# Two copies that spread the rotary table are issued earlier, and their temporaries are held longer

## The chip, the cores and the metric

The kernel runs on one core of a Trainium2 chip. The metric is device time in microseconds (us) of one execution, as the median of several. The core has five engines that each work through a queue of their own, in order: TensorE (PE; its loading of the stationary operand is shown apart as PEld), VectorE (DVE), ScalarE (ACT), GpSimd (POOL) and SyncE (SP), which here issues the transfers. They meet through semaphores alone, so that an instruction that waits holds up everything behind it on its engine.

## The reference

Two decoder layers of the same form run over 512 tokens with 1024 features. In each layer one input projection gives the queries, keys and values of two groups of heads and of an indexer. The first group (kind "a" in the kernel) attends to a sliding window with a learned sink; the second (kind "b") attends only to those keys that the indexer ranks highest, 128 a query. Both groups are projected back, then come a normalisation, a gated feed-forward part with a small second input, and a normalisation.

```python
h = x @ w_in
qa, ka, va, qb, kb, vb, qi, ki, wi = jnp.split(h, cuts, axis=-1)
qa = rope(qa.reshape(B, S, SWA_KV_HEADS, SWA_G, HEAD_DIM), positions)
...
ki = rope(layer_norm(ki, idx_k_g, idx_k_b), positions)
...
sc = jnp.einsum('bqhd,bsd->bqhs', qib, ki).astype(jnp.float32)
idx_score = jnp.einsum('bqhs,bqh->bqs', jax.nn.relu(sc), wib.astype(jnp.float32))
...
_, sel = lax.top_k(idx_score, k_top)
...
mix = jnp.concatenate([oa, ob], axis=-1) @ w_o
x = layer_norm(DN_ALPHA * x + mix, ln1_g, ln1_b)
```

`rope` rotates the two halves of each head by an angle that depends on the token's position and on the feature; its cosines and sines are the rotary table. The table is the same for both layers.

## The kernel before

**Tiles.** The 512 tokens are four blocks (NT = 4) of 128. An fp32 product is made of three fp32r matmuls (`mm3`, L334 to L336) of a high and a low part of each operand. Weights come by SP's transfers into three staging tiles (`wst`); ScalarE rounds each to its high part (L280, L287) and GpSimd subtracts to get the low part (L281, L288), into a ring of five (`wsp`). PSUM has eight banks that go round in a few rings: accumulators, two for transposes (`tp`) and two for scores (`sc`). `t2k()` gives one of twelve temporaries of 128 x 512 fp32, `slot()` one of 28 tiles.

**Start of a layer.** `start()` does, in this order: for each of the four blocks the indexer's projection of 296 columns (`gi_out` rotates its parts, `turns` transposes them, L620 to L622); then for pairs of blocks the projection of 384 columns with keys and values (`kv_out` rotates the keys: a product with the table on VectorE, L520, an addition on GpSimd, L522, a rounding on ScalarE, L525, a subtraction on GpSimd, L526; and copies the values on ScalarE, L613); then `turned_tables()`; then the queries, whose features lie on partitions, so that their rotation (`q_out`, L645) needs the table transposed.

**The table.** `tab64` holds cosines and sines with tokens on partitions and is made once. `turned_tables()` makes the transposed form in each layer: for each of the two halves ScalarE copies 32 columns a block four times side by side into a temporary (L632), PE transposes its four 128 x 128 pieces (L636), and ScalarE copies the bank into the tile `lng` (L637), whose two halves are what `q_out` reads.

**Beside it.** `index()` runs interleaved with `start()`: eight scores a block on PE (L677), a ReLU on ScalarE (L679), a weighted sum on VectorE (L680), for blocks 1 to 3. `topk()` follows, for the same three blocks: 16 rounds each of a maximum of eight (L691) and their replacement (L692) on VectorE, over 256, 384 or 512 keys, 48 rounds a layer. `attention()` runs over units of a block and a group of heads: `scores` (PE L716, VectorE's mask and row maximum L720, ScalarE's exponential L724, the sum's reciprocal on VectorE L730, GpSimd's spreading of it L732) and `values` (transposes of the exponentials L753, transposes of the reciprocals L764, products with the values L747, L772). `rest()` gives the remaining queries and the first part of the output projection (L822, L824 add it to the residual).

**What sets the order.** Several such generators run side by side; each yields an estimate of its cost on PE, and a planner (`order.run`) gives the next turn to the one that is behind by these costs; `order.later` puts transposes off until a due time. From the order in which instructions are issued in this way, a scheduler that knows the tiles' dependencies settles the order on each engine before the kernel runs. A table that is issued at another place thus also changes what stands beside what further on.

Of the kernel before, what the change touches and what calls it, by code (L numbers as in the profile page):

```python
# [20 lines left out]
NT = S // 128  # L21
# [75 lines left out]
def hybrid_kernel(ctx: ExitStack, tc: tile.TileContext, x, p, positions, ln_in_g, ln_in_b, w_in,  # L97
# [3 lines left out]
    PE, V, A, G, SP = nc.tensor, nc.vector, nc.scalar, nc.gpsimd, nc.sync  # L101
# [11 lines left out]
    def bank(tag, bufs, dt=F32):  # L113
        return psum.tile([128, 512], dt, name="bank", tag="bank", bufs=8)

    def acc():
        return bank("acc", 4)
# [4 lines left out]
    def t2k(dt=F32):  # L122
        return tmp.tile([128, 512], dt, name="t2k", tag="t2k")
# [23 lines left out]
    idf = const.tile([128, 128], F32, name="idf")  # L147
# [172 lines left out]
    def w_take():  # L320
        i = wpos["use"]
        if wq[i][0] == "raw":
            i += 1
        wpos["use"] = i + 1
        assert i in w_live, (i, wpos)
        return w_live.pop(i)

    def w_rel():
        wpos["room"] += 1
        w_pump()  # L330

    def mm3(o, sh, sl, mh, ml, start, stop, again=False):

        PE.matmul(o, sh, mh, start=start, stop=False, skip_group_check=again)  # L334
        PE.matmul(o, sh, ml, start=False, stop=False, skip_group_check=again)  # L335
        PE.matmul(o, sl, mh, start=False, stop=stop, skip_group_check=again)  # L336
# [15 lines left out]
    for i in range(4):  # L352
        ps = bank("gb", 4)
# [3 lines left out]
    def tok(t):  # L357
        return slice(t * 128, (t + 1) * 128)
# [30 lines left out]
    def ln_in_sums(t):  # L389
        total, mean = sm(1, "lnsum1"), sm(1, "lnm")  # L390
        A.activation(t2k().bitcast(BF16), xt[t], AF.Copy, accum_out=total)
        A.mul(mean, total, -1.0 / D)
        stats[t] = mean, squares(t, mean)

    def ln_in(t):
        halves = [xt[t][:, h * 512:(h + 1) * 512] for h in range(2)]
        if t == 0:
            mv = sm(2, "bmv")
            for h in range(2):
                ln_stats(t, h)  # L400
            V.bn_aggr(mv, stats.pop(t))
            mean, var, of = mv[:, 0:1], mv[:, 1:2], 1
        else:
            (mean, var), of = stats.pop(t), D
        for h, c in enumerate(halves):
            V.scalar_tensor_tensor(c, c, mean, gb_in[h], op0=OP.add if t else OP.subtract, op1=OP.mult)
        rs = rstd_of(var, of=of)
        for h, c in enumerate(halves):
            last["norm"] = V.scalar_tensor_tensor(c, c, rs, gb_in[2 + h], op0=OP.mult, op1=OP.add).ins
# [24 lines left out]
    def behind(ins, fn):  # L434

        def f(*args):
            with tc.issue_after(ins):
                fn(*args)
        return f

    def to_features(t):
        ts = slice(t * 128, (t + 1) * 128)
        for j in range(KT // 4):
            ps = bank("tp", 2)
            for i in range(4):
                k = 4 * j + i
                PE.transpose(ps[:, i * 128:(i + 1) * 128], xt[t][:, k * 128:(k + 1) * 128], idf)  # L447
            pv = ps.rearrange("p (a n) -> p a n", a=4)
            last["copy"] = A.copy(fh[:, 4 * j:4 * j + 4, ts], pv).ins  # L449
            V.tensor_tensor(fl[:, 4 * j:4 * j + 4, ts], pv, fh[:, 4 * j:4 * j + 4, ts], OP.subtract)  # L450
# [3 lines left out]
    tab64 = const.tile([128, NT, 2, 64], F32, name="tab64")  # L454
# [86 lines left out]
    def take(n):  # L541
        return [w_take() for _ in range(n)]

    def project(ws, n, blocks, lhs, done, rel=0):

        ks = [(i, r, len(w[0])) for i, w in enumerate(ws) for r in range(len(w[0]))]
        ps = [acc() for _ in blocks]
        for k, (i, r, a) in enumerate(ks):
            for o, t in zip(ps, blocks):
                mm3(o[:, :n], *lhs(t, k), ws[i][0][r], ws[i][1][r], k == 0, k == len(ks) - 1)  # L550
            if i < rel and r == a - 1:
                w_rel()
            yield 3 * len(blocks) * 0.218 * n / 512
        for o, t in zip(ps, blocks):
            done(t, o)

    for l in range(L):
# [1 line left out]
        kiT = slot()  # L559
        qiT, qT, work, wi, vt, ma = {}, {}, {}, {}, {}, {}  # L560
        ready = set()
        kin, kmv, turned = {}, {}, []

        def gi_out(t, ps):

# [39 lines left out]
        def kv_out(t, ps):  # L605
# [18 lines left out]
                order.tick(0.4)  # L624
            order.later(D_K, turns)

        def turned_tables():

            cs = const.tile([128, D], F32, name="lng", tag="lng")
            for i in range(2):  # L630
                wide = t2k()
                A.copy(wide.rearrange("p (t n i) -> p t n i", t=NT, n=4),  # L632
                       tab64[:, :, i, None, :32].to_broadcast([128, NT, 4, 32]))
                ps = bank("tp", 2)
                for t in range(NT):
                    PE.transpose(ps[:, tok(t)], wide[:, tok(t)], idf)  # L636
                A.copy(cs[:, i * 512:(i + 1) * 512], ps)  # L637
            return cs[:, :512], cs[:, 512:]

# [193 lines left out]
        def queries(kind, g):  # L833
            ps = [acc(), acc()]
            for k in range(KT):
                if k % 4 == 0:
                    w = w_take()
                for u in range(2):
                    mm3(ps[u], w[0][k % 4][u], w[1][k % 4][u], fh[:, k], fl[:, k], k == 0, k == KT - 1)
                if k % 4 == 3:  # L840
                    w_rel()
                yield 6 * 0.227
            q_out(kind, g, ps)

        def start():
            ws = take(3)
            for t in range(NT):
                if l == 0 or t == 3:
                    to_features(t)
                    yield 0.9  # L850
                if l == 0 and t == 0:
                    with tc.issue_after(last["copy"]):
                        ln_in_sums(2)
                    ln_in_sums(3)
                    for _ in table:
                        pass
                if l == 0 and t + 1 < NT:
                    ln_in(t + 1)
                done = gi_out
                if l == 0 and t + 1 < NT:  # L860
                    done = behind(last["norm"], gi_out)
                if l == 0 and t == 2:
                    with tc.issue_after(last["norm"]):
                        V.tensor_scalar(nsink, sink, -1.0, None, op0=OP.mult)
                yield from project(ws, 296, (t,), from_f, done, 3 * (t == 3))
            ws = take(4)
            for b in ALL:
                yield from project(ws, 384, b, from_f, kv_out, 4 * (b is ALL[-1]))
            turned.extend(turned_tables())
            for q in QS[:NSTART]:  # L870
                yield from queries(*q)

        def rest():
# [5 lines left out]
            for h in range(2):  # L879
                ws = take(2)  # L880
                for b in ALL:
                    yield from project(ws, 512, b, from_ma, res_out(h, ALPHA), 2 * (b is ALL[-1]))

        order.run((start(), 1.0), (index(), 1.0), credit=False)
        order.run((rest(), R_MAIN), (attention(), 1.0), (topk(), R_TOP))
        order.flush()
# [118 lines left out]
        for gi, fs in enumerate(GROUPS):  # L1005
            hs = []
            for f in fs:
# [7 lines left out]
                if gi == 1 and f == fs[0]:  # L1015
                    pT = {}
                    for k in range(2):
                        ps = bank("tp", 2)
# [14 lines left out]
            for h in range(2):  # L1033
                ps = [acc() for _ in range(NT)]
                n = len(hs)
# [13 lines left out]
        for b in TAIL:  # L1049
            for h in range(2):  # L1050
# [4 lines left out]
                ps = [acc() for _ in b]  # L1055
# [52 lines left out]
```

## Time and profile before

| | us |
|---|---|
| median of 3 runs | 1276.74 (1276.61 to 1277.25) |
| the profiled execution | 1275.16 |
| its span, first to last instruction | 1273.4 |
| PE busy in the span | 1223.8 (96%) |
| VectorE busy | 773.4 (61%) |
| GpSimd busy | 677.9 (53%) |
| ScalarE busy | 583.4 (46%) |

The mean clock granted to TensorE is 0.985 of full speed. Busy shares are means over stages that differ: in the page's 40 slices VectorE is between 30% and 90% and above. In the profile, a line such as L636 names the line of the kernel that issued the instruction, `out<-in` names tiles, and the bracket behind an instruction gives the idle time of the engine just before it and what ended it.

### The profile page before, as it was taken

The page shows a single profiled execution, that of the slowest core. Times are in us where ns is not written, and L with a number is a line of the kernel's source. Part 1 is how long each engine was busy: PE and PEld are TensorE (multiplying, and loading weights), DVE is VectorE, ACT ScalarE, POOL GpSimd, SP SyncE. Part 2 cuts the span into 40 slices and gives each one's busy share as a digit, 9 for nine tenths or more (in the row PEclk, how much of TensorE's full clock was granted, in tenths as well). Part 3 has the DMA queues.
Part 4 walks back from the last instruction along what each step waited for, and adds up shares of the span by engine and source line. Part 5 has one row for each costly group of instructions (what it writes and reads, how often), then busy time and mean ns, then how long its engine had stood idle before and what let it go on. Part 6 is the DMA issues. An engine that isn't in the chain of part 4 may idle for free.

```text
span 1273.4 us, 17210 instructions
## 1 busy us (share of the span) xinstructions
PE 1223.8 (96%) x6056; PEld 1006.3 (79%) x6056; DVE 773.4 (61%) x1678; ACT 583.4 (46%) x1185; POOL 677.9 (53%) x523
## 2 busy tenths in 40 slices
PE   7889999999999999999997989999999999999996
PEld 5877667888888888888896867679888888888885
DVE  7689953773636363726677997556736363645365
ACT  6557774443434343434335766843434342434331
POOL 6856632366565656562166645324756575747400
PEclk9989999999999999999998989999999999999998
DMA  5324241343242323034032433204242423231321
GB/s 174 85 82 118 76 155 35 99 131 115 69 132 74 125 77 121 17 116 138 13 91 79 126 90 92 108 27 155 85 132 67 132 79 120 84 99 42 108 83 50
DMA packets 95406, 121.09 MB, mean 95 GB/s; under 512 B 7508, under 2 KB 68180, under 8 KB 95320
## 3 DMA queue, kind: packets, MB, share of 16 engines
q1 hardware_dynamic: 94648, 119.97, 30.4%
q8 instruction: 47, 0.77, 0.3%
q14 instruction: 39, 0.32, 0.1%
q10 hardware_dynamic: 672, 0.03, 0.0%
HBM read 109.49 MB, written 2.10 MB: 88 GB/s over the span
## 4 chain that ended last, share of the span: by engine, by line
PE 83%; DVE 5%; ACT 4%; POOL 4%; issue 2%; DMA 2%; SPq 0%; DVEq 0%; ACTq 0%; POOLq 0%
PE bank L334 25%; PE bank L335 25%; PE bank L336 25%; PE bank L747 2%; PE bank L716 2%; PE bank L753 2%; DMA wst<-in_w_pg_dram 1%; POOL wsp L288 1%; POOL wsp L281 1%; DVE t2k L720 1%; ACT t2k L724 1%; POOL slot L526 1%; PE bank L447 1%; DVE slot L273 1%; PE bank L764 1%
## 5 line engine op out<-in xcount | busy, mean ns | idle before, releaser
L288 POOL TENSOR_TENSOR wsp<-wst,wsp 128x1024 fp32r<-128x1024 f32 (+2 forms) x132 | 313.1, 2385 | 252.2 <-ACT wsp L287 250.2
L335 PE MATMUL bank<-fl,wsp 128*128 128x512 f32 (+1 forms) x896 | 336.0, 376 | 0.4 <-DVE fl L450 0.4
L334 PE MATMUL bank<-fh,wsp 128*128 128x512 f32 (+1 forms) x896 | 335.1, 377 | 1.0 <-ACT fh L449 1.0
L336 PE MATMUL bank<-fh,wsp 128*128 128x512 f32 (+1 forms) x896 | 334.2, 375 | 0.0
L287 ACT CAST wsp<-wst 128x1024 fp32r<-128x1024 f32 (+2 forms) x132 | 134.8, 1030 | 181.2 <-PE bank L336 132.7
L334 PEld LDWEIGHTS bank<-fh,wsp 128*128 128x128 f32 x896 | 168.5, 189 | 31.6 <-ACT fh L449 1.9
L335 PEld LDWEIGHTS bank<-fl,wsp 128*128 128x128 f32 x896 | 169.4, 189 | 30.0 <-DVE fl L450 0.9
L336 PEld LDWEIGHTS bank<-fh,wsp 128*128 128x128 f32 x896 | 169.3, 189 | 29.7
L914 DVE TENSOR_TENSOR t2k<-bank,t2k 128x512 f32<-128x512 f32 x44 | 30.4, 692 | 222.2 <-PE bank L336 222.2
L257 POOL TENSOR_TENSOR wsp<-slot,wsp 128x512 fp32r<-128x512 f32 x100 | 141.4, 1440 | 28.9 <-ACT wsp L256 28.9
L334 PE MATMUL bank<-wsp,slot 128*128 128x512 f32 x392 | 153.3, 391 | 0.0
L335 PE MATMUL bank<-wsp,slot 128*128 128x512 f32 x392 | 152.7, 390 | 0.0
L336 PE MATMUL bank<-wsp,slot 128*128 128x512 f32 x392 | 148.0, 389 | 0.0
L822 DVE TENSOR_TENSOR x<-bank,x 128x512 f32<-128x512 f32 x140 | 91.5, 686 | 88.5 <-PE bank L336 88.5
L944 ACT CAST slot<-t2k 128x256 fp32r<-128x256 f32 (+1 forms) x104 | 49.9, 498 | 143.7 <-DVE t2k L914 102.1
L257 POOL TENSOR_TENSOR wsp<-t2k,wsp 128x512 fp32r<-128x512 f32 x40 | 57.5, 1449 | 92.7 <-ACT wsp L256 92.7
L334 PE MATMUL bank<-wsp,fh 128*128 128x512 f32 (+2 forms) x256 | 92.2, 364 | 1.1 <-ACT fh L449 0.8
L336 PE MATMUL bank<-wsp,fl 128*128 128x512 f32 (+2 forms) x256 | 91.4, 360 | 1.5 <-DVE fl L450 0.8
L335 PE MATMUL bank<-wsp,fh 128*128 128x512 f32 (+2 forms) x256 | 91.5, 357 | 0.0
L334 PEld LDWEIGHTS bank<-wsp,slot 128*128 128x128 f32 x392 | 73.6, 188 | 15.8 <-issue 0.8
L336 PEld LDWEIGHTS bank<-wsp,slot 128*128 128x128 f32 x392 | 73.6, 188 | 15.3
L335 PEld LDWEIGHTS bank<-wsp,slot 128*128 128x128 f32 x392 | 73.6, 188 | 15.0
(163 smaller groups left out, 1971.7 us busy)
## 6 DMA issues: line engine op xcount, KB each, us to landing
wst<-in_w_gu_dram SPq DMA_DIRECT2D x88, 512.0 KB, 3.5
slot<-in_w_down_dram SPq DMA_DIRECT2D x80, 256.0 KB, 2.9
wst<-in_w_in_dram SPq DMA_DIRECT2D x16, 512.0 KB, 3.5
wst<-in_w_o_dram SPq DMA_DIRECT2D x16, 512.0 KB, 3.9
slot<-t2k SPq DMA_DIRECT2D x128, 64.0 KB, 2.0
wst<-in_w_pg_dram SPq DMA_DIRECT2D x16, 512.0 KB, 4.1
wst<-in_w_in_dram SPq DMA_DIRECT2D x8, 256.0 KB, 2.9
lng<-in_ln_g_dram SPq DMA_DIRECT2D x4, 512.0 KB, 3.9
```

Source lines behind the costliest of these rows:

```text
L257: G.tensor_tensor(w[:, 1, j], src[j], w[:, 0, j], OP.subtract)
L287: A.copy(w[:, 0, :a * n], st[:, :a * n])
L288: G.tensor_tensor(w[:, 1, :a * n], st[:, :a * n], w[:, 0, :a * n], OP.subtract)
L334: PE.matmul(o, sh, mh, start=start, stop=False, skip_group_check=again)
L335: PE.matmul(o, sh, ml, start=False, stop=False, skip_group_check=again)
L336: PE.matmul(o, sl, mh, start=False, stop=stop, skip_group_check=again)
L716: PE.matmul(ps[:, o:o + nn], qT[kind, g][j][:, tok(t)], kT[c, s][:, k0:k0 + nn], start=(s == 0), stop=(s == 1))
L747: PE.matmul(o[u * 64:(u + 1) * 64], vt[b0 + b][:, c * 64:(c + 1) * 64], pts[b][:, u], start=b == 0, stop=b == nb - 1)
L753: PE.transpose(ps[:, j * 128:(j + 1) * 128], es[j][:, b * 128:(b + 1) * 128], idf)
L822: V.tensor_tensor(xt[t][:, c], ps, xt[t][:, c], OP.add)
L914: V.tensor_tensor(a, ps[1, f], a, OP.mult)
L944: A.copy(h[0], src)
```

## The change

The two copies of a layer move out of `turned_tables()` into a new function `wide_tables()`, which `start()` calls once block 1's indexer projection has been issued. The two temporaries they write are kept in a list until `turned_tables()` transposes them. What is copied, transposed and copied back stays the same. Lines from 634 on stand four lower in the changed kernel (L636 is L640, L691 is L695), and those behind the call six.

```diff
@@ -559,7 +559,7 @@
-        kin, kmv, turned = {}, {}, []
+        kin, kmv, turned, wide = {}, {}, [], []
@@ -624,16 +624,20 @@
+        def wide_tables():
+
+            for i in range(2):
+                wide.append(t2k())
+                A.copy(wide[i].rearrange("p (t n i) -> p t n i", t=NT, n=4),
+                       tab64[:, :, i, None, :32].to_broadcast([128, NT, 4, 32]))
+
         def turned_tables():
 
             cs = const.tile([128, D], F32, name="lng", tag="lng")
             for i in range(2):
-                wide = t2k()
-                A.copy(wide.rearrange("p (t n i) -> p t n i", t=NT, n=4),
-                       tab64[:, :, i, None, :32].to_broadcast([128, NT, 4, 32]))
                 ps = bank("tp", 2)
                 for t in range(NT):
-                    PE.transpose(ps[:, tok(t)], wide[:, tok(t)], idf)
+                    PE.transpose(ps[:, tok(t)], wide[i][:, tok(t)], idf)
                 A.copy(cs[:, i * 512:(i + 1) * 512], ps)
             return cs[:, :512], cs[:, 512:]
@@ -863,6 +867,8 @@
                 yield from project(ws, 296, (t,), from_f, done, 3 * (t == 3))
+                if t == 1:
+                    wide_tables()
```

Two places show what this does to the order on an engine. First, ScalarE's queue in layer 0. Before, the copies (L632) stand at the end of the key and value projections, between the keys' roundings:

```order
L613 COPY slot<-bank 128x64
L525 CAST slot<-t2k 128x128
L525 CAST slot<-t2k 128x2x128
L613 COPY slot<-bank 128x128
L632 COPY t2k<-tab_117 128x512 x2
L613 COPY slot<-bank 128x64
L525 CAST slot<-t2k 128x128
L637 COPY lng<-bank 128x512 x2
```

In the changed kernel they stand (L631) right behind the copies that build the table and the castings of the features, ahead of the next weight tile:

```order
L497 COPY tab_118<-t2k 128x4x16
L498 COPY tab_118<-t2k 128x4x16
L449 CAST fh<-bank 128x4x128 x3
L631 COPY t2k<-tab_117 128x512 x2
L287 CAST wsp<-wst 128x768 x2
L280 CAST wsp<-wst 128x16x2x32
```

And at the old place the copies out of the transposes' banks (L641) move up, ahead of the last keys' roundings:

```order
L622 COPY slot<-bank 128x128 x12
L280 CAST wsp<-wst 128x16x2x32
L525 CAST slot<-t2k 128x2x128
L613 COPY slot<-bank 128x128
L641 COPY lng<-bank 128x512 x2
L613 COPY slot<-bank 128x64
L683 ACTIVATE bank<-bank 128x384
L525 CAST slot<-t2k 128x128
```

Here the copies have gone from between the roundings, and only one rounding (L525) is left between the index transposes' copies (L622) and the tables' (L641).

The second place is VectorE's queue where, in layer 0, the first windowed scores (L720, `win`) come among the rounds of top-k (L691 and L692, over 384 keys there). Before:

```order
L691 MAX m_1835<-work_802 128x8
L720 ISA t2k,ng<-bank,win,nsink 128x128
L720 ISA ng 128x1
L692 MATCH_REPLACE work_802<-m_1835,work_802 128x384
L720 ISA t2k,ng<-bank,win,nsink 128x128
L720 ISA ng 128x1
L720 ISA t2k,ng<-bank,win,nsink 128x256
L720 ISA ng 128x1
L691 MAX m_1865<-work_802 128x8
```

After:

```order
L696 MATCH_REPLACE work_806<-m_1658,work_806 128x384
L695 MAX m_1679<-work_806 128x8
L696 MATCH_REPLACE work_806<-m_1679,work_806 128x384
L724 ISA t2k,ng<-bank,win,nsink 128x128
L724 ISA ng 128x1
L695 MAX m_1726<-work_806 128x8
L696 MATCH_REPLACE work_806<-m_1726,work_806 128x384
L724 ISA t2k,ng<-bank,win,nsink 128x128
L724 ISA ng 128x1
L724 ISA t2k,ng<-bank,win,nsink 128x256
```

A whole round now stands between the first two windowed rows where half a one stood. Of the layer's 48 rounds, 26 stand ahead of the first windowed row before and 20 now (25 and 20 in layer 1), and 44 ahead of the last one before, 41 now (44 and 43 in layer 1).

## The prediction

> **What bounds the kernel now.** I read the first part of the page, then PE's waits summed over the span, then PE's timeline at the greatest of them. The lines give start, length, engine, line and what is done; the bracket holds the idle time ahead and what ended it.
>
> ```profile
> span 1273.4 us, 17210 instructions
> PE 1223.8 (96%) x6056; PEld 1006.3 (79%) x6056; DVE 773.4 (61%) x1678; ACT 583.4 (46%) x1185; POOL 677.9 (53%) x523
> ...
> PE bank L636 <- ACT t2k L632: 16.1, 2, 8.4
> PE bank L764 <- POOL rb L732: 6.8, 3, 3.8
> ```
>
> PE is busy for 96% of the span, so over the whole span its work is the bound and only PE's waits can be won. The largest, 16.1 us in two pieces, is the table transposes (L636) waiting for the copies that the change moves (L632). Its two places, one a layer:
>
> ```profile
> 57.29 1.13 PE L620 MATMUL bank<-idr,slot 128*128 128x128 f32 x12
> 66.86 1.97 PE L636 MATMUL bank<-idf,t2k 128*128 128x128 f32 x8 [8.44 <-ACT t2k L632]
> ...
> 680.25 0.44 PE L677 MATMUL bank<-slot 128*128 128x384 f32 x1 [0.86 <-DVE work L680]
> 688.40 1.97 PE L636 MATMUL bank<-idf,t2k 128*128 128x128 f32 x8 [7.71 <-ACT t2k L632]
> ```
>
> Why the copies are late stands in ScalarE's and GpSimd's timelines:
>
> ```profile
> 65.30 0.82 ACT L525 CAST slot<-t2k 128x128 fp32r<-128x128 f32 x2 [2.23 <-POOL t2k L522]
> 66.18 1.14 ACT L632 COPY t2k<-tab 128x512 f32<-128x512 f32 x2
> ...
> 59.64 4.67 POOL L281 TENSOR_TENSOR wsp<-wst,wsp 128x1024 fp32r<-128x1024 f32 x2
> 64.95 0.73 POOL L522 TENSOR_TENSOR t2k<-t2k 128x64 f32<-128x64 f32 x2
> ```
>
> The copies read a table that has long been there. They stand in ScalarE's queue behind the keys' roundings (L525); those wait for the rotary additions (L522) on GpSimd, and those stand behind two halves of a weight tile (L281) that hold GpSimd to 64.31. PE waits for a queue, not for data.
>
> The stall costs more than its length. The windows give, per stretch, its length, busy time of PE, PEld, DVE, ACT and POOL, then the granted clock:
>
> ```profile
> 58.42:66.86 8.44, 0.00 (x1) 0.00 (x1) 8.10 (x28) 5.59 (x23) 8.38 (x9) 0.68 0.77 222
> 66.86:71.50 4.64, 4.64 (x15) 4.07 (x16) 4.30 (x14) 1.95 (x5) 0.80 (x3) 0.50 0.11 40
> 680.69:688.40 7.71, 0.01 (x2) 0.01 (x1) 7.33 (x26) 4.87 (x19) 7.38 (x8) 0.63 0.71 206
> 688.40:693.00 4.60, 4.60 (x15) 4.03 (x16) 4.29 (x14) 1.95 (x5) 0.80 (x3) 0.50 0.12 41
> ...
> 228.89 0.87 PE bank L447 x8
> ```
>
> Behind each stall PE has half its clock for 4.6 us: eight such transposes take 1.97 us there and 0.87 at full clock (last row, from the chain of waits). Half of 4.64 and of 4.60 is 2.3 us a layer lost once more.
>
> **The change, part by part.** *The two copies, early.* They take 1.14 us together, in each layer. In the new order they stand between ScalarE's castings of the features (L449) and its next weight tile (L287), where it now idles:
>
> ```profile
> 36.48 0.84 ACT L287 CAST wsp<-wst 128x768 fp32r<-128x768 f32 x1 [6.47 <-PE bank L336]
> 658.99 0.84 ACT L287 CAST wsp<-wst 128x768 fp32r<-128x768 f32 x1 [5.15 <-PE bank L336]
> ```
>
> 1.14 fits in 6.47 and in 5.15: nothing, and were the cover gone it would be 1.14 us on a weight tile, 2.3 in both layers. The table is done by then, since the rotary copies stand ahead of them. *The two temporaries* out of a ring of twelve: ten others serve the projections meanwhile, and their users are not PE. I take nothing; what it costs if a rotary product must wait for a free one is bounded by that product's GpSimd chain, 0.73 us a layer.
>
> *The transposes.* What is late next in layer 0 is the PSUM bank, whose earlier readers are the scores (L680) and the copies of the index transposes (L622):
>
> ```profile
> 58.81 0.61 DVE L680 SCALAR_TENSOR_TENSOR work<-bank,wi,causal 128x384 f32<-128x384 f32 x1
> 679.97 2.12 ACT L622 CAST slot<-bank 128x128 fp32r<-128x128 f32 x12
> ```
>
> L680 ends at 59.42, 1.0 us into the stall, so 7.4 of 8.44 goes. In layer 1 PE ends L677 at 680.69, and a third of the twelve copies has been done by then; I find nothing later and take 7.7. With the cold clock: 8.44 − 1.0 + 2.3 = 9.8 us, and 7.7 + 2.3 = 10.0. **If PE keeps all of it, 19.8 us.** Nothing behind the transposes should take their place: the next thing that needs the slow chain is the keys' own transposes.
>
> ```profile
> 79.26 1.16 PE L620 MATMUL bank<-idr,slot 128*128 128x128 f32 x12
> ...
> 67.72 0.46 POOL L526 TENSOR_TENSOR slot<-t2k,slot 128x128 fp32r<-128x128 f32 x1 [0.51 <-ACT slot L525]
> ```
>
> Their last input is there at 68.18; 9.8 us earlier PE is at them at 69.5 or later (six more matmuls are ahead of them in the new order).
>
> *What VectorE gives back.* PE then comes 10 us earlier into the stretch where top-k (48 rounds of L691 and L692 in a layer) shares VectorE with the attention scores, which PE waits for. How full VectorE is (third figure behind the length), and what it waits for in 58 to 157, then in 680 to 781:
>
> ```profile
> 84.00:104.00 20.00, 20.00 (x91) 16.57 (x90) 19.64 (x43) 12.51 (x20) 16.52 (x11) 1.00 0.46 130
> 104.00:157.00 53.00, 48.98 (x284) 35.85 (x283) 51.03 (x168) 41.24 (x126) 30.31 (x45) 0.97 0.29 83
> 728.00:781.00 53.00, 47.50 (x269) 34.79 (x268) 49.56 (x161) 38.94 (x121) 27.23 (x43) 0.94 0.25 73
> ...
> DVE work L680 <- ACT bank L679: 4.2, 5, 3.1
> DVE t2k L720 <- PE bank L716: 1.3, 5, 0.4
> ...
> DVE t2k L720 <- PE bank L716: 2.5, 6, 0.9
> DVE work L680 <- ACT bank L679: 1.8, 3, 1.1
> ```
>
> VectorE is 98%, 96% and 94% busy there. Work that is in line ahead of the last windowed score row cannot be done faster; that row can come earlier only by rounds that change sides and by idle time that is filled. Rounds and their prices:
>
> ```profile
> L691 DVE MAX8 m<-work 128x8 f32<-128x384 f32 x32 | 17.8, 557 | 0.4
> L692 DVE MATCH_REPLACE8 work<-m,work 128x384 f32<-128x384 f32 x32 | 17.4, 545 | 0.0
> L691 DVE MAX8 m<-work 128x8 f32<-128x512 f32 x32 | 22.1, 690 | 0.2
> L692 DVE MATCH_REPLACE8 work<-m,work 128x512 f32<-128x512 f32 x32 | 21.7, 678 | 0.0
> L692 DVE MATCH_VALUE_LOAD work<-m,work 128x8 f32 x96 | 8.5, 89 | 1.8
> ```
>
> A round of 384 keys is 0.56 + 0.55 + 0.09 = 1.19 us, one of 512 is 1.46. Counted in the two instruction orders, 44 rounds stand ahead of the last windowed row before, and 41 (layer 0) and 43 (layer 1) now, those of 512 keys. That is 3 × 1.46 = 4.4 and 1.5 us earlier. To it comes idle time. Layer 0 has 4.2 + 1.3 = 5.5 us: all but the limit would be 9.9, more than PE's 9.8. I choose that the one wait of 3.1 us at L680 gets filled, since rounds for the first blocks are still open then, and the other 2.4 stays: 9.9 − 2.4 = 7.5 us. Layer 1 has 2.5 + 1.8 = 4.3, limit 5.8; the waits of L720 for PE vanish, since VectorE is now the later of the two, 1.1 of L680's is filled, and 0.7 stays: 5.1. **Sum: 7.5 + 5.1 = 12.6 us.** Bounds: VectorE fills none of its idle time, 4.4 + 1.5 = 5.9; all of it, 9.8 + 5.8 = 15.6; PE does not feel VectorE, 19.8. I take the middle value, since VectorE's rows are nearest to full and PE's rows there are 90 to 92% busy, not 100. What is given back should show at the row transposes of the reciprocals (L764), behind the reciprocal chain (L720, exponentials, L730 on VectorE, L732):
>
> ```profile
> 112.72 0.69 PE L764 MATMUL bank<-idf,rb 128*128 128x128 f32 x2 [2.26 <-POOL rb L732]
> 735.70 0.69 PE L764 MATMUL bank<-idf,rb 128*128 128x128 f32 x2 [3.81 <-POOL rb L732]
> 112.72:114.00 1.28, 1.28 (x6) 1.06 (x8) 1.18 (x3) 1.28 (x4) 0.10 (x1) 0.50 0.42 102
> 114.00:116.00 2.00, 2.00 (x9) 1.24 (x8) 1.80 (x7) 1.90 (x6) 0.51 (x2) 0.50 0.59 171
> ```
>
> Both waits leave half a clock behind already (0.50 in the last two rows), so a longer wait adds its length but no second cold phase.
>
> [...]
>
> **The rivals.** *PE keeps all* (19.8 us, median 1256.9): the 2% to 6% of time in which VectorE isn't busy take in more than I say, or PE has enough other matmuls to run ahead. For it: PE has out-projection and query work that it can place anywhere; against it: VectorE is at 96% from 104 to 157. *VectorE gives most back* (5.9 us, 1270.8): the idle time of VectorE are gaps of handing over between engines that no earlier start fills. For it: a wait of 1.3 us in 5 pieces is of that kind; against: the 3.1 us piece. *Slower*: more top-k rounds get ahead of the first reciprocal in each layer, because the scores come earlier than the rounds end; each round of 384 delays L730, and with it L764, by 1.19 us. It decides from (19.8 + 2.6) / 2 / 1.19 = 9.4 more rounds a layer; with 11 a layer, 26.2 − 19.8 = 6.4 us is lost, 1283. For it: L764 is PE's second wait already; against: the orders have only one to three rounds more between the first windowed row and its reciprocal. *No change*: the stall comes again at the next wait of PE, 1276.7. Against it: 68.18 for the last input, above, and only the bank that ends at 59.42.
>
> **How the numbers follow.** The profiled execution took 1275.16 us (span 1273.4 and 1.76 around it), 1.58 less than the median of 1276.74. 1275.16 − 12.6 = 1262.6, and against the median 1276.74 − 12.6 = 1264.1: that is the predicted time. Chances: this forecast 0.54, its own range 1261.1 to 1267.5 (15.6 us saved, and 9.2, half way from 12.6 to the lower bound of 5.9); all kept 0.18; most given back 0.20; slower 0.05; no change 0.03. The range takes in the bounds of VectorE's part and nearly reaches the case of all 19.8: 1257 to 1271.5. About 0.2% (2.6 us) is what a measurement of this kernel tells from none. Faster by more than that: the first three, less a little for the third's low end and copies without cover, 0.90; within it 0.05; slower 0.05.
>
> **What would show it.** Right: L636's line (now four lines lower) has gone from PE's waits or is about 1 us in layer 0 alone; granted clock 1.00 in the 5 us behind the transposes; the moved copies in an idle gap of ScalarE with L287 no later; the index transposes near 70 us; the wait at L764 grown by 2 to 3 us in layer 0 and about 5 in layer 1; top-k ending earlier by the filled idle time. Wrong: PE still ahead by 19 to 20 us at 157 us and in the end (all kept), or L764's waits grown by 6 us and more in each layer (most given back); a wait of PE for L680 or for a PSUM bank where L636 waited.

## The result, and the profile after

| | before | after |
|---|---|---|
| median of 4 runs | 1276.67 us (1275.01 to 1277.25) | 1257.68 us (1257.35 to 1259.14) |
| profiled execution | 1275.16 | 1257.35 |
| its span | 1273.4 | 1255.6 |
| mean granted clock of the profiled execution | 0.985 | 0.992 |

The ratio of the times is 0.9856, 95% interval 0.9838 to 0.9873: 18.4 us faster (16.2 to 20.7). The profiled spans differ by 17.8 us. The forecast was 1264.1 with a range of 1257 to 1271.5; the time lies in it, near its fast end, but outside the 1261.1 to 1267.5 to which the forecast's own chance of 0.54 belonged. It is nearest to the rival that PE keeps all (1256.9). The saving of 12.6 us was too small by some 6.

First the page's part on engines, and PE's waits summed over the span (total, times, longest):

```profile
span 1255.6 us, 17205 instructions
PE 1218.7 (97%) x6056; PEld 1002.7 (80%) x6056; DVE 766.5 (61%) x1678; ACT 580.9 (46%) x1185; POOL 678.2 (54%) x523
...
PE bank L768 <- POOL rb L736: 7.2, 4, 4.0
PE bank L751 <- ACT t2k L759: 4.7, 7, 1.2
...
PE bank L640 <- DVE work L684: 1.0, 1, 1.0
...
PE bank L640 <- ACT slot L622: 0.6, 1, 0.6
```

The table transposes (now L640) wait 1.6 us in all where they waited 16.1. The span less PE's busy time is PE's idle time: 49.6 us before, 36.9 now. Of the 17.8 us, 12.7 are thus idle time (14.5 off this wait, some given back at others) and 5.1 are shorter busy time of the same 6056 matmuls. An estimate of the clock's part is 2.9: in the stretches at half clock PE is busy for 17.9 us before and for 12.1 now, and half of the difference is saved. The other 2.2 were not traced. The places, in PE's and ScalarE's timelines:

```profile
59.34 1.09 PE L640 MATMUL bank<-idf,t2k 128*128 128x128 f32 x8 [1.05 <-DVE work L684]
70.82 1.14 PE L620 MATMUL bank<-idr,slot 128*128 128x128 f32 x12
672.64 1.09 PE L640 MATMUL bank<-idf,t2k 128*128 128x128 f32 x8 [0.62 <-ACT slot L622]
...
29.75 1.14 ACT L631 COPY t2k<-tab 128x512 f32<-128x512 f32 x2
36.36 0.84 ACT L287 CAST wsp<-wst 128x768 fp32r<-128x768 f32 x1 [5.46 <-PE bank L336]
645.82 1.15 ACT L631 COPY t2k<-tab 128x512 f32<-128x512 f32 x2
```

And windows behind the transposes, then the half-clock stretches that are left while PE works (length; PE, PEld, DVE, ACT, POOL busy; clock; DMA):

```profile
59.34:64.00 4.66, 4.66 (x25) 3.99 (x26) 4.45 (x16) 3.98 (x15) 4.66 (x3) 1.00 0.72 192
672.64:677.30 4.66, 4.66 (x25) 4.01 (x26) 4.46 (x14) 4.18 (x15) 4.44 (x3) 1.00 0.72 188
...
105.03:108.45 3.42, 3.33 (x16) 2.91 (x14) 3.38 (x12) 2.06 (x7) 1.05 (x2) 0.50 0.75 266
135.75:139.17 3.42, 3.42 (x17) 2.77 (x14) 3.42 (x12) 2.38 (x12) 1.31 (x5) 0.50 0.45 145
716.02:717.49 1.47, 0.00 (x1) 0.01 (x1) 1.42 (x6) 1.47 (x4) 0.98 (x5) 0.50 0.60 138
717.49:722.85 5.36, 5.36 (x23) 4.38 (x24) 5.20 (x17) 3.15 (x10) 1.01 (x2) 0.50 0.48 162
```

The transposes run at full clock (eight in 1.09 us at 1.00, where they took 1.97 at 0.50 before). One half-clock stretch is new: that at 135.75, in layer 0.

The gain by layers stands in PE's timeline at a group of transposes of features at the start of layer 1, and in VectorE's at the last values of its attention, before and after:

```profile
641.43 1.03 PE L447 MATMUL bank<-idf,x 128*128 128x128 f32 x8
...
837.63 0.42 DVE L772 TENSOR_TENSOR t2k<-bank,t2k 128x256 f32<-128x256 f32 x1 [0.65 <-PE bank L747]
```

```profile
633.54 1.03 PE L447 MATMUL bank<-idf,x 128*128 128x128 f32 x8
...
819.87 0.42 DVE L776 TENSOR_TENSOR t2k<-bank,t2k 128x256 f32<-128x256 f32 x1 [0.65 <-PE bank L751]
```

Layer 1 starts 7.9 us earlier than before and its attention ends 17.8 us earlier. So layer 0 gained 7.9 us where the forecast had 7.5, and layer 1 gained 9.9 where it had 5.1. Nearly the whole error is in layer 1: VectorE was to hold PE back there, and did not. The first reciprocals, where this was to be seen, come earlier by nearly all of the gain (102.81 for 112.03 in layer 0), and the wait for them has hardly grown:

```profile
103.49 0.44 PE L768 MATMUL bank<-idf,rb 128*128 128x128 f32 x2 [2.85 <-POOL rb L736]
717.49 0.69 PE L768 MATMUL bank<-idf,rb 128*128 128x128 f32 x2 [3.97 <-POOL rb L736]
...
93.03 0.35 DVE L724 CUSTOM_DVE_ANT_0 t2k<-bank,win,nsink 128x128 f32<-128x128 f32 x1 [0.53 <-PE bank L720]
706.48 0.35 DVE L724 CUSTOM_DVE_ANT_0 t2k<-bank,win,nsink 128x128 f32<-128x128 f32 x1 [0.77 <-PE bank L720]
```

2.85 for 2.26 and 3.97 for 3.81, where 2 to 3 us and about 5 more were to come. VectorE waits for PE at the first windowed score rows (last two lines, 0.53 and 0.77): it is not late there. It was not late in the kernel before either:

```profile
104.43 0.35 DVE L720 CUSTOM_DVE_ANT_0 t2k<-bank,win,nsink 128x128 f32<-128x128 f32 x1 [0.41 <-PE bank L716]
725.59 0.35 DVE L720 CUSTOM_DVE_ANT_0 t2k<-bank,win,nsink 128x128 f32<-128x128 f32 x1 [0.28 <-PE bank L716]
```

These rows come 11.4 us earlier in layer 0, and in layer 1 19.1 us earlier, 11.2 of them its own.

### The profile page after: what moved, and what is told of

It reads as the page before. It is cut to its first block, busy times and chain, and to the rows that moved or that the text cites. A ratio compares the mean times of both kernels' runs of the same rounds, so it can differ in the third digit from the quotient of the medians.

```text
span 1255.6 us, 17205 instructions
## 1 busy us (share of the span) xinstructions
PE 1218.7 (97%) x6056; PEld 1002.7 (80%) x6056; DVE 766.5 (61%) x1678; ACT 580.9 (46%) x1185; POOL 678.2 (54%) x523
## 4 chain that ended last, share of the span: by engine, by line
PE 84%; DVE 5%; ACT 4%; POOL 3%; issue 2%; DMA 2%; SPq 0%; DVEq 0%; ACTq 0%; POOLq 0%
PE bank L334 25%; PE bank L335 25%; PE bank L336 25%; PE bank L751 3%; PE bank L720 2%; PE bank L757 2%; DMA wst<-in_w_pg_dram 1%; POOL wsp L288 1%; ACT t2k L728 1%; DVE work L696 1%; DVE t2k L724 1%; DMA wst<-in_w_in_dram 1%; POOL slot L526 1%; PE bank L447 1%; DVE m L695 1%
## 5 line engine op out<-in xcount | busy, mean ns | idle before, releaser
L287 ACT CAST wsp<-wst 128x1024 fp32r<-128x1024 f32 (+2 forms) x132 | 134.6, 1029 | 180.8 <-PE bank L336 130.3
L335 PEld LDWEIGHTS bank<-wsp,slot 128*128 128x128 f32 x392 | 73.6, 188 | 15.1
```

Source lines behind the costliest of these rows:

```text
L287: A.copy(w[:, 0, :a * n], st[:, :a * n])
```

## The experiments

The question was why VectorE, busy for 94% to 98% of these stretches, gave nothing back in layer 1. Theory A at the start: what gates PE is VectorE's queue at the first windowed rows and the first reciprocal, where the new order lets 6 and 5 rounds fewer ahead, not at the last windowed row. Rivals: layer 1's gain hangs on an alignment; VectorE does not gate PE at all.

**One layer at a time.**

```diff
...
-                if t == 1:
+                if t == 1 and l == 0:
                     wide_tables()
```

and the same with `l == 1`; the other layer makes its copies at the old place.

> The copies go early in layer 0 alone; layer 1 keeps them at the old place. The change as a whole took 17.8 us off the span, 7.9 of it up to the end of layer 0 and 9.9 behind it. Theory A (each layer's gain is its own: stall and cold clock go, and VectorE gates PE only at the first reciprocal): 7.9 us less than the kernel before, about 1268.8; layer 1 waits again 7 to 8 us at the table transposes. Theory B (part of layer 1's gain is a lucky alignment that layer 0's earlier end brings, such as the L694 mask that took 2.53 us in layer 1 before and 0.36 after): 10 us or more less, 1266.7 or below, with L694 short in layer 1 too.

Measured: 1269.41 us, 0.9943 (0.9928 to 0.9957), 7.5 us less in the medians where 7.9 was expected.

> The copies go early in layer 1 alone. Theory A: 9.9 us less than the kernel before, about 1266.8, and layer 0 as before with its 8.4 us wait. The prediction's step for layer 1 (VectorE at the last windowed score row gives 5 of 10 us back): 5.1 us less, 1271.6. Theory B (alignment from layer 0): 5 to 8 us less, 1268.7 to 1271.7.

Measured: 1270.36 us, 0.9942 (0.992 to 0.9964), 6.5 us less; but its four runs lie apart. The profiled one took 1265.29 at a mean clock of 0.989, and its span of 1263.5 is the 9.9 us below before that theory A has; the three others took 1270.35 to 1270.66 at 0.984. 0.005 of clock over the span is 6 us. By an estimate from these clocks the three had some 10 us more at half clock; only the profiled run has a trace, so where they had it stays open, and the run does not decide between 9.9 and 5.1 by its median. Its order in layer 1 is also not quite that of the changed kernel: 41 rounds stand ahead of the last windowed row, where 43 do. In the run with layer 0 alone, layer 1's transposes wait 8.21 us again; in that with layer 1 alone, layer 0's 8.39. From layer 0 alone to both the profiled spans fall by 11.9 us (1267.5 to 1255.6), some of it, by an estimate, the clock's, whose mean in these two executions is 0.987 and 0.992.

**More rounds ahead of the first windowed row.** In the changed kernel:

```diff
+            with tc.issue_after(rounds[31]) if kind == "a" and t == g == j == 0 else nullcontext():
                 V.tensor_tensor_reduce(es[j], ps[:, o:o + nk], mask, ...)
...
```

> The changed kernel, with the first windowed score row of each layer ordered behind the 32nd of top-k's 48 rounds (the order has 33 rounds ahead of it, and 34 ahead of the first reciprocal, where the changed kernel has 20 and 26). Theory A (VectorE's queue sets the first reciprocal, and this wait of PE is the gate that the earlier start ran into): the reciprocal comes 6 rounds of 384 keys and 2 of 512 later, 6 x 1.19 + 2 x 1.46 = 10 us a layer, less 2 to 3 us of idle time that is filled, so 5 to 8 us a layer if no other matmuls fill it: 1265 to 1273, with PE's waits in the attention's first 15 us grown by as much, unless PE's order puts projection matmuls there, which then are missing later. Rival (VectorE's queue does not gate PE at all, the wait at the reciprocal's transposes is the latency of the chain): within 1.5 us of 1257.7.

Measured: 1282.71 us, 25 more than the changed kernel and slower than before, 1.0043 (1.0029 to 1.0057): above what was expected, which had priced the eight rounds at the reciprocal and not the 13 at the first row. The profiled run, the fastest of five, took 1277.33. PE's waits for VectorE's rows in it (scores L723, rows L728) in all, and the first one:

```profile
PE bank L723 <- DVE ng L728: 24.8, 10, 9.6
...
107.92 1.22 PE L723 MATMUL bank<-slot 128*128 128x256 f32 x4 [9.36 <-DVE ng L728]
```

So VectorE's queue can gate PE, and it does it at the windowed rows as soon as enough rounds stand ahead of them. The rival that VectorE never counts is out.

**No rounds between the first windowed row and its reciprocal.**

```diff
+                    if 16 * (t - 1) + r == 20:
+                        yield from wait("recip")
+                    with tc.issue_after(last["recip"]) if 16 * (t - 1) + r == 20 else nullcontext():
                         V.max(m8, w)
...
```

> The changed kernel, with top-k's rounds from the 21st on held until the first reciprocal of the layer is done, so that no round stands between the first windowed score row and this reciprocal (26 before it in the changed kernel, 20 here). Theory A: PE's waits at the reciprocal's transposes (3.0 us in layer 0, 4.2 in layer 1) shrink below 1 us each, and the half clock behind them goes (3.4 us in layer 0 and 5.4 in layer 1 at half speed, 1.7 and 2.7 us); top-k ends 5 to 7 us later, where 30 us of slack lay before: 5 to 11 us less than the changed kernel, 1247 to 1253. Rival (latency of the chain): the waits stay at 2 us or more and the time within 1.5 us of 1257.7. If top-k's later end is what counts, slower than 1259.

Measured: 1256.65 us, 0.9844 (0.9829 to 0.986): 1.0 less than the changed kernel, with overlapping intervals. Six rounds are gone from the chain, 7 us of VectorE, but the waits at the reciprocal's transposes (L774 here) have only fallen to 4.3 us from 7.2:

```profile
101.40 0.44 PE L774 MATMUL bank<-idf,rb 128*128 128x128 f32 x2 [0.91 <-POOL rb L742]
106.56 0.50 PE L723 MATMUL bank<-slot 128*128 128x256 f32 x2 [1.73 <-DVE ng L727]
715.75 0.69 PE L774 MATMUL bank<-idf,rb 128*128 128x128 f32 x2 [2.69 <-POOL rb L742]
```

More than half of the wait is thus latency of the chain, and what goes here comes back elsewhere: PE's waits for the score rows are 4.7 us in all, where the changed kernel has 0.7. Theory A's 5 to 11 us was wrong: taking these rounds out gains no more than 1.0 us, which is within the spread.

**All rounds ahead of the last windowed row.**

```diff
+            end = (kind, t, g, j) == ("a", 3, 1, 3)
+            while end and len(rounds) < 48:
+                next(tk)
+            with tc.issue_after(rounds[47]) if end else nullcontext():
                 V.tensor_tensor_reduce(es[j], ps[:, o:o + nk], mask, ...)
...
```

> The changed kernel, with the last windowed score row of each layer ordered behind all 48 rounds of top-k (41 and 43 in the changed kernel), the first one as before behind 20 or 21. The prediction's step (VectorE's work ahead of the last windowed row limits PE): 7 rounds of 512 keys in layer 0 and 5 in layer 1 come ahead of it, 12 x 1.46 = 17.5 us, less up to 7 us of idle time filled: 10 to 17 us more than the changed kernel, 1268 to 1275. Theory A (VectorE gates PE at the first windowed rows and their reciprocal alone; behind them PE has projection matmuls to run): 0 to 4 us more, 1257 to 1262.

Measured: 1277.33 us, 1.0005 (0.9996 to 1.0015) against the kernel before, 19.7 more than the changed kernel. PE's new waits, at the transposes of the exponentials (L763 here):

```profile
149.02 0.69 PE L763 MATMUL bank<-idf,t2k 128*128 128x128 f32 x2 [6.09 <-ACT t2k L734]
772.33 0.69 PE L763 MATMUL bank<-idf,t2k 128*128 128x128 f32 x2 [3.88 <-DVE work L698]
```

Theory A said 0 to 4, and falls in this form: rounds put ahead of the last row cost their full length too. That row comes at 147.86 for 136.34 in layer 0 and at 771.16 for 752.29 in layer 1, 11.5 us later and 8.4 of its own, for 7 and 5 rounds of 1.46 us (10.2 and 7.3). VectorE has no room to spare at either row. The prediction's rule of prices was sound here; what has to be explained is why the change did not run into it.

**Half of top-k's rounds left out**, in the kernel before and in the changed one:

```diff
-                for _ in range(TOPK // 8):
+                for _ in range(TOPK // 16):
```

> The kernel before with 8 rounds of top-k a block in place of 16 (the second half of the selection is left out). It serves as the base of the next run. VectorE has some 33 us a layer less to do, so PE's waits at the reciprocal's transposes (2.3 and 3.8 us) with the half clock behind them should go: 5 to 12 us less than the kernel before, 1265 to 1272; the two waits at the table transposes stay at 7 to 9 us each.

Measured: 1282.42 us, 1.0049 (1.0033 to 1.0064): slower than with all rounds, not 5 to 12 us faster. PE's waits at the reciprocal are 2.9 us longer in it and its mean clock is 0.981; why the order comes out worse with less work was not followed up.

> The changed kernel with 8 rounds of top-k a block in place of 16 (the same part left out). With VectorE off the path the change is worth the stalls and their half clock alone, by the prediction's sum 9.8 + 10.0 = 19.8 us less than the kernel before with 8 rounds. Theory A: 18 to 21 us less. If the stall's price itself was too high in the prediction: 16 us or less. If PE's waits at the reciprocal are the latency of the chain rather than VectorE's queue, they stay as in the changed kernel (7 us in all).

Measured: 1256.76 us, 0.9853 (0.983 to 0.9875). That is 25.7 us below the same kernel without the change, more than the 18 to 21 expected; 5.4 of them are what that base is slower than the kernel before with all rounds. It is within 1 us of the changed kernel with all rounds, and the intervals overlap. The profiled run is the slowest of its four (1260.73, the others 1254.98 to 1257.0). PE's waits in each, of before first:

```profile
PE bank L636 <- ACT t2k L632: 16.1, 2, 8.4
PE bank L764 <- POOL rb L732: 9.7, 4, 4.6
...
PE bank L768 <- POOL rb L736: 7.1, 4, 3.2
PE bank L720 <- DVE ng L724: 3.9, 7, 1.2
```

Half the rounds, 24 in a layer and some 29 us of VectorE (8 each of 0.92, 1.19 and 1.46 us), are taken away, and neither kernel gets faster by it. The sum of VectorE's work is therefore not what bounds PE. For the waits at the reciprocal, which stay (9.7 for 6.8 us, 7.1 for 7.2), the run is a weaker test than it looks, because the order was made anew. Counted in the traces of the changed kernel, 17 and 16 of the 24 rounds (layers 0 and 1) still stand ahead of the first windowed row, where 20 stood, and 4 between it and the reciprocal, where 6 stood; what the rounds cost there is shown by the run further up that takes all six out. In the kernel before, 18 and 17 stand ahead of that row for 26 and 25, and in layer 0 it starts at 104.00 for 104.43: eight rounds fewer, and hardly sooner.

So the rounds act as filler: the order gives them time in which VectorE would be idle, which is why VectorE is nearly full and still not late. Put ahead by force, they are paid at once.

This gives theory C: the order on VectorE was made anew for the earlier scores and let fewer rounds ahead of them, at the first row above all; that is why VectorE had nothing to give back. The run that tells:

**The old counts in the changed kernel.** 26 (25 in layer 1) rounds ahead of the first windowed row and 44 ahead of the last one.

```diff
+            ahead = {(0, 0, 0): 26 - l, (3, 1, 3): 44}.get((t, g, j), 0) if kind == "a" else 0
+            while len(rounds) < ahead:
+                next(tk)
+            with tc.issue_after(rounds[ahead - 1]) if ahead else nullcontext():
                 V.tensor_tensor_reduce(es[j], ps[:, o:o + nk], mask, ...)
...
```

> The changed kernel, with as many rounds of top-k ahead of the windowed score rows as the kernel before had: 26 (25 in layer 1) ahead of the first row and 44 ahead of the last one, where the changed kernel has 20 and 41 (43). Theory C (the rounds fill VectorE's idle time and cost nothing as long as the order, made anew for the earlier scores, lets fewer of them ahead; put ahead by force they are paid in full): of the run with 13 more rounds ahead of the first row, 10 us a layer, some 5 us were slack; here 6 and 5 more at the first row cost 1 to 3 us a layer, and 3 and 1 more at the last row 4.4 and 1.5 us, together 6 to 10 us more than the changed kernel, 1264 to 1268. Rival (the old counts themselves are harmless, and the two runs before were slow because all rounds were forced): within 2 us of 1257.7.

Measured: 1267.95 us, 0.9937 (0.9917 to 0.9956): 10.3 more than the changed kernel, 8.3 less than the kernel before. More than half of the change's gain goes when VectorE keeps its old counts. PE's waits show what holds it, the transposes of the exponentials (L763 here) and the scores (L722), both behind VectorE's rows (L730):

```profile
PE bank L763 <- ACT t2k L734: 8.0, 6, 3.9
PE bank L722 <- DVE ng L730: 7.1, 10, 1.5
```

The changed kernel has 0.4 and 0.7 us there. At the reciprocal the waits fall, to 2.5 us from 7.2. Where the delay begins, in VectorE's timeline:

```profile
99.61 0.56 DVE L697 MAX8 m<-work 128x8 f32<-128x384 f32 x1
100.09 0.33 DVE L730 CUSTOM_DVE_ANT_0 t2k<-bank,win,nsink 128x128 f32<-128x128 f32 x1
...
718.10 0.56 DVE L697 MAX8 m<-work 128x8 f32<-128x384 f32 x1
718.57 0.33 DVE L730 CUSTOM_DVE_ANT_0 t2k<-bank,win,nsink 128x128 f32<-128x128 f32 x1
```

The first windowed row is at 100.09 for 93.03: 7.1 us later, six rounds of 1.19, and it follows a round without idle time. In layer 1 it is at 718.57 for 706.48, of which 6.6 us come from layer 0: 5.5 us, close to five rounds (6.0). From there to the end of its attention layer 0 adds nothing (6.5 us late at its last values), so the three rounds more at the last row, 4.4 us, are hidden behind the 7.1 that were lost at the first; layer 1 loses 3.8 of its own. The delay at the first row, which the prediction had not priced, is large enough for the whole loss. What the last row's count alone would cost, this run cannot tell, since its delay is covered; seven and five rounds there cost their length, above.

**Cover for the reciprocal's wait.** The changed kernel, with the planner's charge behind the attention's second unit raised:

```diff
-LAG, FILL = dict(a=1, b=2), {2: 6, 5: -2}
+LAG, FILL = dict(a=1, b=2), {2: 9, 5: -2}
```

> The changed kernel, with the planner charging the attention 9 in place of 6 behind its second unit, so that more projection matmuls stand in PE's order behind the first reciprocal (the second reciprocal's transposes have 165 of them ahead where 144 stood). Theory (PE's waits at the reciprocal's transposes are a latency that other matmuls could cover): as the first reciprocal keeps its place, the first waits (2.9 and 4.0 us) stay, and only the later small ones go: 0 to 3 us less than 1257.7. If the matmuls are missing later: up to 5 us more.

Measured: 1263.57 us, 0.99 (0.9881 to 0.9918), 5.9 more than the changed kernel; PE's waits at the reciprocal are 8.6 us for 7.2. The first reciprocal's transposes have 144 projection matmuls ahead of them as in the changed kernel; the added ones stand only behind them, where they do not cover its wait. What else makes it slower was not followed up.

> The same with 12 in place of 6: 184 projection matmuls stand ahead of the first reciprocal's transposes, where 144 stood (40 more, 9 us of PE). If PE's first waits are a latency that other matmuls cover, the two waits (2.9 and 4.0 us) and the half clock behind them (1.7 and 2.7 us) go: up to 11 us less, 1247. But these matmuls are then missing in the rest of the attention, where its waits come back: between 5 us less and 5 us more than 1257.7.

Measured: 1252.06 us, 0.981 (0.9793 to 0.9827): 5.6 less than the changed kernel, with intervals that do not touch, and the fastest here. PE's page row and waits:

```profile
PE 1216.4 (97%) x6056; PEld 1000.8 (80%) x6056; DVE 767.9 (61%) x1678; ACT 579.0 (46%) x1185; POOL 678.2 (54%) x523
...
PE bank L768 <- POOL rb L736: 1.8, 3, 1.1
...
92.50:147.00 54.50, 49.52 (x294) 37.13 (x293) 52.78 (x175) 41.51 (x126) 32.69 (x46) 1.00 0.35 101
```

With 40 projection matmuls more ahead of the first reciprocal's transposes in layer 0 (184 for 144), and 34 more in layer 1, their waits fall from 7.2 to 1.8 us, and the half clock behind the first one goes (1.00 in the stretch that had 0.94). PE's own work covers the wait. A setting of 9 is worse than 6, and 12 better: one step does not show the direction.

**The temporaries.** Ten in the ring for twelve (`NSLOT, NTMP = 28, 10`), and the table made once, kept for layer 1, also with ten:

```diff
-                if t == 1:
+                if t == 1 and l == 0:
                     wide_tables()
...
-            turned.extend(turned_tables())
+            if l == 0:
+                turned.extend(turned_tables())
...
```

> The changed kernel with 10 temporaries in the ring in place of 12, for the whole run: the price of the two temporaries that the change holds, taken for good. The prediction took nothing for holding them: within 1.5 us of 1257.7 if that is right also without any release. If it costs, it bears on the run with the table made once, which had 10 as well and took 1258.72: what this run takes over 1257.7 is what making the table once gained there beside its loss of 1 us.

Measured: 1260.37 us, 0.9876 (0.986 to 0.9892), 2.7 more than the changed kernel.

> The changed kernel, with the transposed table made once in layer 0 and kept for layer 1 (its own tile of 4 KB a partition; two temporaries fewer, 10 in the ring, to make room). Layer 1 loses eight transposes (0.87 us at full clock), the wait ahead of them (0.6 us) and 1.14 + 1.2 us on ScalarE: 1 to 2 us less than the changed kernel, 1255.5 to 1257, if two temporaries fewer cost nothing; above 1258.5 they cost something.

Measured: 1258.72 us, 0.9865 (0.9847 to 0.9882). Against the run above, the table made once gains 1.7 us, less than the 2.7 us that two temporaries fewer cost for the whole run. Both differences are small, and the intervals overlap; the single runs with ten temporaries alone (1260.24 to 1260.44) do lie apart from those with the table made once (1258.35 to 1259.4) and from those of the changed kernel (1257.35 to 1259.14). The change holds the two only from 30 to 59 us in layer 0 and from 646 to 673 in layer 1, and nothing in PE's waits names them there.

## Why the prediction was right in its range and wrong in its size

- **What bounds, and the stall: right.** PE waited for a queue. The wait went from 8.44 to 1.05 us in layer 0, behind L684 (L680 before), as the prediction had it (1.0), and from 7.71 to 0.62 in layer 1, where it had nothing: the copies of the index transposes (L622) end a little later than PE's scores. 14.5 us for 15.1.
- **The half clock: right.** The 4.64 and 4.60 us at half clock are at 1.00 now, 2.3 us a layer. That a longer wait at the reciprocal adds no more half clock was the author's estimate. The stretches there keep 3.42 and 6.83 us (3.41 and 6.82 before) as the waits grow by 0.6 and 0.2 us; in the run with 32 rounds ahead of the first row, with a wait of 9.36 us at its scores, the clock is at 0.50 all through the 12 us from 106 to 118.
- **The copies: right.** 1.14 and 1.15 us in ScalarE's idle time, with 5.46 and 4.11 us of it left ahead of L287.
- **No next stall: right.** The keys' transposes come at 70.82 without a wait.
- **The held temporaries: right as far as the runs go.** Nothing in PE's waits names them; for a hold of the whole run they would cost some 2.7 us.
- **What VectorE gives back: wrong, and it is the error.** The step is "Work that is in line ahead of the last windowed score row cannot be done faster; that row can come earlier only by rounds that change sides and by idle time that is filled", with its limit of 5.8 us in layer 1 and the sum 7.5 + 5.1. It read VectorE's busy share as a limit where it was the filler's: half the rounds taken away move the changed kernel by 0.9 us, within its spread. The warning stood in the profile before, where VectorE waits for PE at the first windowed row of both layers. And it counted only at the last row, 3 and 1 rounds. At the first row the order has 6 and 5 fewer, 7.1 and 6.0 us, and with the idle time filled ahead of it (VectorE's idle time from its first round to there is 3.9 and 1.4 us less) the same rule would have let that row come 11.0 us earlier in layer 0, more than PE's 9.8, and 7.3 us in layer 1; it came 11.4 and 11.2 earlier. Giving the old counts back takes 10.3 us off the gain and leaves 8.3; the step's idle part alone, 12.6 − 4.4 − 1.5 = 6.7, is not far from that.
- **The limit at the last row was also too low by its own rule.** These rows, of before and then after, are the last windowed ones of each layer:

```profile
145.14 0.47 DVE L720 CUSTOM_DVE_ANT_0 t2k<-bank,win,nsink 128x256 f32<-128x256 f32 x1
768.23 0.48 DVE L720 CUSTOM_DVE_ANT_0 t2k<-bank,win,nsink 128x256 f32<-128x256 f32 x1
```

```profile
136.34 0.47 DVE L724 CUSTOM_DVE_ANT_0 t2k<-bank,win,nsink 128x256 f32<-128x256 f32 x1
752.29 0.47 DVE L724 CUSTOM_DVE_ANT_0 t2k<-bank,win,nsink 128x256 f32<-128x256 f32 x1
```

  They come 8.8 us earlier in layer 0 (forecast 7.5) and 15.9 − 7.9 = 8.0 in layer 1 (5.1, limit 5.8). Two terms were missing in layer 1, 3.4 us together: top-k starts 1.2 us earlier within it (first maximum at 671.55 for 680.64), and one instruction was 2.2 us longer before, beside a subtraction on GpSimd (last section). Whether that second one is worth anything to PE was not shown: in the run with layer 0 alone it takes 0.29 us, and that layer 1 is no faster than before; how long it runs at half clock there is open. From the last row to the end of the attention PE gains another 1.8 us in layer 1 and loses 0.9 in layer 0, so the row was no gauge of PE either.
- **Layer 0's 7.9 for 9.8.** 0.6 us are the longer wait at the first reciprocal, 1.7 the new half-clock stretch (3.42 us at half), which follows waits of 0.23 and 1.18 us at 132.6 and 134.5. 9.8 − 2.3 = 7.5 is the forecast's number, but by another sum: its 2.3 us less were to be idle time that VectorE keeps. That layer 0 came out near the forecast is luck.
- **The rivals.** "PE keeps all" (19.8 us, 0.18) is nearest to what happened. "Slower" by rounds ahead of the reciprocal can be made: 13 rounds more ahead of the first row by force, 8 more ahead of the reciprocal, gave 1282.71. That this is near the 1283 priced for 11 ahead of the reciprocal is luck too.

What stays open: why layer 0's second half-clock stretch starts, where the runs with layer 1 alone had theirs, why the kernel before gets slower with half the rounds, and what the old count at the last row would cost alone.

## What to carry to other kernels

When an engine next to the bound is full, look at what fills it: if it is work with slack that the order puts wherever there is room, its busy share is no limit, and only the waits of the bound engine for it are. Count what stands ahead of the first instruction that the bound engine waits for, and not only of the last one. And a wait that looks like a queue may be mostly a latency: taking the queue's work out of the chain is the test, with a count of what really went from ahead of the wait.

## What the runs showed of the hardware

**A VectorE instruction that started beside a GpSimd one lasted until that one had ended.** In the kernel before, layer 1:

```profile
698.66 2.40 POOL L281 TENSOR_TENSOR wsp<-wst,wsp 128x1024 fp32r<-128x1024 f32 x1 [8.95 <-ACT wsp L280]
...
698.68 2.53 DVE L694 TENSOR_SCALAR work<-work 128x256 f32<-128x256 f32 x1
...
77.02 0.29 DVE L694 TENSOR_SCALAR work<-work 128x256 f32<-128x256 f32 x1
...
60.69 0.43 DVE L691 MAX8 m<-work 128x8 f32<-128x256 f32 x1
```

The same instruction takes 0.29 us with GpSimd at rest (third line; GpSimd is idle from 68.18 to 77.46) and 2.53 when it starts 0.02 us behind a subtraction of 2.40, whose end at 701.06 it outlasts by 0.15. The price here is 2.2 us. Top-k's maxima kept their time: the last line, 0.43 us, stands inside a 4.67 us pair of such subtractions that began at 59.64, and one of the same form at 695.93, with GpSimd idle, takes 0.43 too. Why the one was held and the others were not, the trace does not show.

**The clock fell to half behind short waits too, and in pieces of 3.41 us.** In the changed kernel a stretch of 3.42 us at half clock begins at 135.75, behind two waits of 1.4 us together; behind three waits of 0.26 to 0.58 us between 142 and 150 in the kernel before the clock stayed at 1.00 (142 to 157). What decides between the two is not shown. The half-clock stretches in which PE works are 3.42, 3.42 and 6.83 us long in the changed kernel (the last from 716.02 to 722.85), and 10.24, 3.41, 10.23 and 6.82 in the kernel before (from 61.50, 112.70, 682.74 and 733.94): one, two or three times 3.41. Their starts lie whole pieces apart: 15 from 61.50 to 112.70, nine from 105.03 to 135.75. And the time of one kernel moved with the clock: of the four executions with the change in layer 1 alone, one took 1265.29 us at a mean clock of 0.989 and three took 1270.35 to 1270.66 at 0.984.
